# A two-layer decoder trunk on one core: output projection in 512 + 256 columns, sum of squares on GpSimd, two orders changed

## The chip, the core and the metric

The kernel runs on one core of a Trainium2 chip. A core has five engines that work side by side, each through its own queue: TensorE (PE; its weight loads are shown apart, as PEld), VectorE (DVE), ScalarE (ACT), GpSimd (POOL) and SyncE (SP), which here only issues DMAs. Matmuls read SBUF and write PSUM; DVE and ACT read both. The metric is the device time of one execution in microseconds, lower being better.

## The reference

The input x is 256 tokens of 1024 channels, float32. Each of two layers is a feed-forward block, a token mixer and a second feed-forward block, each on the RMS-normalised x and added back to it:

```python
def hybrid_layer(x, ...):
    x = x + 0.5 * swiglu(rms_norm(x, ffn1_norm), ffn1_w_gate_up, ffn1_w_down)
    h = rms_norm(x, mix_norm)
    z = h @ w_in                       # 512 pool, 3 x 512 attention, 2 x 1024 gate channels
    ...
    y_pool = multiscale_pool(u, pool_w, pool_scale)
    q = rope(rms_norm(q.reshape(B, S, N_HEADS, HEAD_DIM), q_norm))
    k = rope(rms_norm(k.reshape(B, S, N_HEADS, HEAD_DIM), k_norm))
    y_attn = moba_attention(q, k, v)
    gates = jax.nn.sigmoid(gl + b_gate).reshape(B, S, N_BRANCH, D)
    merged = gates[:, :, 0] * (y_pool @ w_branch_pool) + gates[:, :, 1] * (y_attn @ w_branch_attn)
    x = x + merged @ w_out
    x = x + 0.5 * swiglu(rms_norm(x, ffn2_norm), ffn2_w_gate_up, ffn2_w_down)
    return x
```

With 256 tokens there is one attention block, so the attention is a causal softmax over all keys, with 8 heads of 64. The hidden width of a feed-forward block is 2816.

## The kernel before

**Layout.** x lies as channels on 128 partitions by 256 tokens, in 8 columns of 128 channels (`x[:, f, :]`, f = 0 to 7; the tile is called `gx`). Weights stream from memory in units of 128 x 2048 float32 (`fetch`, line 96): one DMA on SP into `raw` (four buffers), then `split` (line 114) for each half: ACT writes the rounded high part `hi` (L115), DVE the remainder `lo` (L116). Six buffers each of `hi` and `lo` hold three units.

**Products.** Every float32 product is made from split operands in three terms: high weight by high data, high weight by low data, low weight by high data. Data that is split lies as `[P, 2, S]`, high half and low half side by side. `chain` (line 134) makes a product in two matmuls: the high weight by both halves (512 columns, the two results kept in two halves of a PSUM bank), and the low weight by the high half (256 columns, added to the first half). Its result is spread over two halves that a drain adds up. `chain3` (line 139) makes it in three matmuls of 256 columns that all add into one half.

**Order.** The order on PE is that of the program (`keep`). On the other engines a planner orders instructions by the program and by when their operands are ready.

**The norm.** RMS normalisation is taken out of the products: `prep(f, ...)` (line 237) is called for each column of x when it is finished. `split_x` writes the split column times its gain into `hx` (L225 on ACT, L226 on DVE), and `square_x` (line 228) squares it on ACT (L234) and adds it to `acc` on DVE (L235). `factor_spread` (line 274) splits `acc` into `ar` (`halves`, L187 and L188), sums it over the partitions with two matmuls (`ss`, L283) and takes the reciprocal root; the results are scaled later. A block that follows the mixer runs twelve steps of `columns` (four matmuls each) before `ss`, seven of them before column 7 of `hx` is needed. In the mixer, `factor` does the same with another matmul (`st`), after the first quarter of the projections.

**The start.** The first block takes its first three units in small pieces as they arrive (lines 682 to 697), and `pairs` (line 172) walks over them together, two rows of weights at a time. A row of `columns` (line 146) makes, for j = 0 and 1, a high and a low product.

**Attention.** Eight `gate` steps (line 491), each 32 matmuls over one weight unit, carry the attention between them (loop at line 602). `score_two` writes the scores of two pairs of heads into two PSUM tiles `sc`; on its second call, in the middle of `gate(4)`, it first writes the values' products of the first two pairs into a free part of the same two tiles (`ys`, `values_two`). `soften` runs `softmax` (line 428) on one `sc`: mask, maximum, exponential on ACT, and scaling by the sums (L448), which gives `pr`. `heads_end` (line 560) takes a values' product out of PSUM as a high half (L562, ACT) and a low half (L563, DVE) into `yk`, part of the tile `ax`. `turn_two` (line 581) allocates two tiles `pt`, which take over the buffers of `sc` (two buffers in this stage), then runs on PE four `pool_map` matmuls in each (on its second call) and six transposes of `pr` in each (L455).

**After the gates.** `branch` and `mixed` make the gated sum and split it into `mk` (`halves`). `project` (line 668) multiplies it by the output weights: eight columns f of eight products, the first three columns taken six products ahead. It then adds the column to x (L676, DVE) and calls `after(f)`, which is `prep` of the next block. Each column has a PSUM tile `ps` of two halves (`quarter`, four buffers), of which the first half is used.

`add_x` (line 359) drains a column of the down projection, made by `chain`: an ACT copy of the second half (L363), a DVE addition of it to x (L364), and a DVE addition of the first half out of PSUM (L365).

Of the kernel before, what the change touches and what calls it, by code (L numbers as in the profile page):

```python
# [18 lines left out]
F32 = mybir.dt.float32  # L19
F32R = mybir.dt.float32r  # L20
AF = mybir.ActivationFunctionType
OP = mybir.AluOpType
# [3 lines left out]
P = 128  # L26
D = 1024
S = 256
L = 2
NK = D // P  # L30
# [18 lines left out]
def trunk_kernel(ctx: ExitStack, tc: tile.TileContext, x_in, w_in, pw_in, qkn_in, rope_in, mask_in, band_in, out):  # L49
    nc = tc.nc  # L50
# [6 lines left out]
    small = ctx.enter_context(tc.tile_pool(name="small", bufs=4))  # L57
# [3 lines left out]
    def quarter(name):  # L61
        return pat.tile([P, 2, S], F32, name=name, tag="at")
# [10 lines left out]
    act = nc.scalar.activation  # L73
    tt = nc.vector.tensor_tensor
# [3 lines left out]
    def mm(*args, **kw):  # L78
        return keep(nc.tensor.matmul(*args, **kw))  # L79

    def banks(pool, name):

        return pool.tile([P, 2, 2, S], F32, name=name, tag="mm" if pool is pmm else "at2")
# [6 lines left out]
    def unit():  # L90

        if not ahead:
            fetch()
        return ahead.pop(0)
# [23 lines left out]
    def blk(z, b, n=1):  # L118

        size = z[0].shape[-1]  # L120
        c = b * P % size
        return z[b * P // size][:, c:c + n * P]

    def steps(z):

        if len(z.shape) == 3:
            z = z.rearrange("p a s -> p (a s)")
        return z.rearrange("p (s a c) -> p a s c", a=4, c=4)

    def prod(ps, w, xk, first, last):  # L130

        return mm(steps(ps), lhsT=w, rhs=steps(xk), start=first, stop=last)

    def chain(ps, hi, lo, b, xk, first, last):

        prod(ps, blk(hi, b), xk, first, False)
        return prod(ps[:, 0, :], blk(lo, b), xk[:, 0, :], False, last)

    def chain3(ps, hi, lo, b, xs, first=True, last=True):

        for i, xk in enumerate(xs):
            prod(ps, blk(hi, b + i), xk[:, 0, :], first and i == 0, False)
            prod(ps, blk(hi, b + i), xk[:, 1, :], False, False)
            prod(ps, blk(lo, b + i), xk[:, 0, :], False, last and i == len(xs) - 1)

    def columns(w, ps, ks):

        for k in ks:
            for j in range(2):
                chain(ps[j] if isinstance(ps, list) else ps[:, j], *w, 2 * k + j, hk[k], k == 0, k == NK - 1)  # L150

    def pair(w, t, other=None, at=0):

        ps = banks(pmm, "ps")
        columns(w, ps, range(at))
        if other:
            other()
        columns(w, ps, range(at, NK))
        drain(t, ps)
# [3 lines left out]
    def drain(t, ps):  # L163
        act(t, ps[:, :, 1, :], AF.Copy)  # L164
        drained.append(tt(t, ps[:, :, 0, :], t, op=OP.add))  # L165
# [6 lines left out]
    def pairs(ws, ts):  # L172

        pss = [banks(pmm, "ps"), banks(pmm, "ps"), *([quarter("pe") for _ in range(2)] for _ in ts[2:])]
        for k0 in range(0, NK, 2):
            for w, ps in zip(ws, pss):
                columns(w, ps, (k0, k0 + 1))
        for t, ps in zip(ts[:2], pss):
            drain(t, ps)
        for t, ps in zip(ts[2:], pss[2:]):  # L180
            for j, pe in enumerate(ps):
                act(t[:, j, :], pe[:, 1, :], AF.Copy)
                tt(t[:, j, :], pe[:, 0, :], t[:, j, :], op=OP.add)
# [9 lines left out]
    x = gx[:, L * NG:L * NG + NK * S].rearrange("p (k s) -> p k s", s=S)  # L193
# [25 lines left out]
    hk = [hx[:, k] for k in range(NK)]  # L219
    acc = acts.tile([P, S], F32, name="acc")  # L220

    def split_x(f, l, col):

        g = gain[:, l, col + f:col + f + 1]
        act(hx[:, f, 0, :], x[:, f, :], AF.Copy, scale=g)  # L225
        stt(hx[:, f, 1, :], x[:, f, :], g, hx[:, f, 0, :].bitcast(F32), op0=OP.mult, op1=OP.subtract)  # L226

    def square_x(f):

        if f == 0:  # L230
            act(acc, x[:, f, :], AF.Square)
        else:
            sq = small.tile([P, S], F32, name="sq", tag="sq", bufs=2)
            act(sq, x[:, f, :], AF.Square)  # L234
            tt(acc, acc, sq, op=OP.add)  # L235

    def prep(f, l, col):
        split_x(f, l, col)
        square_x(f)

    def rsqrt(r, ss, inv):

# [140 lines left out]
    def normed(pt, rt, name):  # L383
        z = acts.tile([P, 2, GW], F32, name=name, **({"tag": "v"} if name == "v" else {"tag": "tok", "bufs": 2}))
        for t in range(2):
            act(z[:, t, :], pt[:, t], AF.Copy, scale=rt[:, t:t + 1])
        return z
# [78 lines left out]
    def by_half(z):  # L466
        return z.rearrange("p (i c) -> p i c", c=P)

    def mix(l, after):
# [6 lines left out]
        k = normed(pt, rt, "k")  # L476
# [14 lines left out]
        def gate(f, *other):  # L491
            pair(unit(), gates[f], *other)
            fetch()

        def open_gate(f):
            tt(gates[f], gates[f], bc2(r), op=OP.mult)  # L496
            for j in range(2):
                c = j * NK + f
                act(gates[f][:, j, :], gates[f][:, j, :], AF.Tanh, scale=0.5, bias=hb[:, c:c + 1])
# [60 lines left out]
        def heads_end(p, y):  # L560

            act(by_half(yk[p][:, 0, :]), y, AF.Copy)  # L562
            tt(by_half(yk[p][:, 1, :]), y, by_half(yk[p][:, 0, :]).bitcast(F32), op=OP.subtract)  # L563
# [3 lines left out]
        scs, ys, prs = [], [], []  # L567
# [4 lines left out]
        def score_two(p):  # L572

            scs[:] = [flat("sc") for _ in range(2)]
            if p:
                ys[:] = [sc[:, :, rest] for sc in scs]
                values_two(0, ys)
            for i, sc in enumerate(scs):
                scores(qT, kT, p + i, sc)

        def turn_two(p, gs=()):

            pts = [flat("pt") for _ in range(2)]
            for g, pt in zip(gs, pts):
                pool_map(g, pt[:, :, rest])
            for pr, pt in zip(prs, pts):
                by_key(pr, pt)
            for pT, pt in zip(pTs[p:], pts):
                act(pT[:, :, :3 * P], pt[:, :, :3 * P], AF.Copy)
            for g, pt in zip(gs, pts):  # L590
                map_end(g, pt[:, :, rest])
            prs.clear()
# [6 lines left out]
        def soften(i, pin=False):  # L599
            prs.append(softmax(scs[i], pin))  # L600

        for h in range(NH):
            gate(h, *((lambda: score_two(h // 2), NK // 2) if h % 4 == 0 else ()))
            if h == 4:
                for i in range(2):
                    soften(i, i > 0)
                for p, y in enumerate(ys):
                    heads_end(p, y)
            elif h < 2:
                soften(h)  # L610
            elif h % 4 == 2:
                turn_two(h // 4 * 2, (0, 1) if h > 4 else ())
            elif h == 3:
                pool_diff()
            open_gate(h)
# [15 lines left out]
        ws = [unit() for _ in range(2)]  # L631
        two = [banks(pmm, "two") for _ in range(2)]
        sums = {0: two[0][:, 0], 2: two[1][:, 0]}
# [4 lines left out]
        ys = [y[:, :, :P] for y in both]  # L638
# [11 lines left out]
        mk = acts.tile([P, NK, 2, S], F32R, name="mk", tag="ga")  # L650
        mk = [mk[:, i] for i in range(NK)]
# [14 lines left out]
        ws, sums = [], []  # L666

        def project(f, k0=0, k1=NK):
            if f % 2 == k0 == 0:
                ws.append(unit())  # L670
            if k0 == 0:
                sums.append(quarter("ps"))
            ps = sums[f][:, 0]
            chain3(ps, *ws[f // 2], f % 2 * 8 + k0, mk[k0:k1], k0 == 0, k1 == NK)
            if k1 == NK:
                tt(x[:, f, :], ps, x[:, f, :], op=OP.add)  # L676
                after(f)

        for step in ((0, 0, 6), (1, 0, 6), (2, 0, 6), (0, 6), (1, 6), (2, 6), *((f,) for f in range(3, NK))):
            project(*step)  # L680
# [17 lines left out]
    for f in range(NK):  # L698
        square_x(f)
    n_unit[0] = len(w3)  # L700
    ahead.extend(w[1:] for w in w3)
    for l in range(L):
        ffn(lambda f: prep(f, l, C_GM), len(w3) if l == 0 else 0)
        if l == 0:
            for d, z in ((rope, rope_in), (mask, mask_in), (qkn, qkn_in)):
                nc.sync.dma_start(d, z)
        mix(l, lambda f: prep(f, l, C_G2))
        if l + 1 < L:
            ffn(lambda f: prep(f, l + 1, C_G1))
        else:  # L710
            ffn(lambda f: nc.sync.dma_start(out[:, f, :], x[:, f, :]), end=True)
# [90 lines left out]
```

## Time and profile before

| | |
|---|---|
| median of three runs | 1003.99 us (1003.69 to 1004.67) |
| profiled execution | 1004.1 us |
| its span, first to last instruction | 1002.2 us |
| granted TensorE clock | 1.000 |
| busy: PE, PEld | 997.2 us, 906.0 us |
| busy: DVE, ACT, POOL | 793.1 us, 619.5 us, 1.5 us |
| read from memory | 190.82 MB, 191 GB/s over the span |

Busy time of PE contains waiting inside its pipeline, so a busy PE alone proves nothing; its starts and the chain of work that ended last say more. In the timelines a row is: start in us, length in us, engine, line, operation, what it writes and reads, how many were merged, and in brackets how long the engine had been idle and what released it. In the groups, the numbers behind the bar are busy time, mean length in ns of one, and idle time before them with what ended it. In the chain of work a row is start, length, engine, tile, line and count. In a list of waits it is the total, the number and the longest.

### The profile page before, as it was taken

What the parts mean: (1) busy time and instruction counts of PE and PEld (TensorE: products, weight loads), DVE (VectorE), ACT (ScalarE), POOL (GpSimd) and SP (SyncE); (2) the same over time, 40 slices, a digit from 0 to 9 for tenths busy, and PEclk for the clock granted to TensorE, in tenths of its full rate; (3) what the DMA queues carried; (4) which work ended last, traced back from release to release, by engine and by line L of the source; (5) the groups of instructions that cost most, each with busy time, mean ns of one, the idle gap of its engine ahead of it and who ended that gap; (6) DMA issues with size and microseconds to landing.
All of it is one profiled execution on the core that took longest, in us unless ns stands there. A gap on an engine that the chain in (4) does not pass through costs nothing.

```text
span 1002.2 us, 16011 instructions
## 1 busy us (share of the span) xinstructions
PE 997.2 (100%) x6348; PEld 906.0 (90%) x6348; DVE 793.1 (79%) x1195; ACT 619.5 (62%) x981; POOL 1.5 (0%) x26
## 2 busy tenths in 40 slices
PE   9999999999999999999999999999999999999998
PEld 8888899898899998888889999888989999888898
DVE  6998866698978888886688888666989888888752
ACT  7866655557756666665575666556677567666541
POOL 0000000000000000000000000000000000000000
PEclk9999999999999999999999999999999999999999
DMA  8866655643546665565556566555545465565640
GB/s 294 314 210 210 209 186 195 221 157 146 191 139 210 207 212 174 206 210 189 193 190 212 184 209 206 183 201 191 188 176 172 131 215 202 187 204 198 205 152 22
DMA packets 30170, 192.89 MB, mean 192 GB/s; under 512 B 3344, under 2 KB 4624, under 8 KB 7568
## 3 DMA queue, kind: packets, MB, share of 16 engines
q1 hardware_dynamic: 30096, 191.88, 56.1%
q8 instruction: 49, 0.80, 0.3%
q14 instruction: 25, 0.20, 0.1%
HBM read 190.82 MB, written 1.05 MB: 191 GB/s over the span
## 4 chain that ended last, share of the span: by engine, by line
PE 97%; DVE 2%; DMA 0%; issue 0%; ACT 0%; SPq 0%
PE ps L79 83%; PE pt L79 7%; PE two L79 4%; PE pe L79 1%; PE sc L79 1%; DVE lo L116 1%; PE pt L455 1%; PE y L79 1%; DMA raw<-w 0%; PE tp L417 0%; DVE gates L165 0%; DVE gates L496 0%; DVE nb L438 0%; PE st L79 0%; DVE uT L538 0%; DVE gates L522 0%
## 5 line engine op out<-in xcount | busy, mean ns | idle before, releaser
L79 PE MATMUL ps<-hx,hi 128*128 128x512 f32 x1696 | 568.5, 383 | 0.4 <-ACT hi L115 0.4
L116 DVE TENSOR_TENSOR lo<-raw,hi 128x1024 fp32r<-128x1024 f32 (+2 forms) x372 | 440.1, 1187 | 136.1 <-ACT hi L115 130.9
L115 ACT ACTIVATE hi<-raw 128x1024 fp32r<-128x1024 f32 (+2 forms) x372 | 381.5, 1031 | 242.9 <-PE ps L79 185.2
L79 PE MATMUL ps<-hx,lo 128*128 128x256 f32 x1696 | 463.3, 273 | 0.0
L79 PEld LDWEIGHTS ps<-hx,hi 128*128 128x128 f32 x1696 | 318.5, 188 | 57.4 <-ACT hi L115 0.7
L79 PEld LDWEIGHTS ps<-hx,lo 128*128 128x128 f32 x1696 | 318.8, 188 | 0.2 <-DVE lo L116 0.2
L79 PE MATMUL ps<-ga,hi 128*128 128x512 f32 (+1 forms) x264 | 87.0, 376 | 0.0
L79 PE MATMUL ps<-gc,hi 128*128 128x512 f32 (+1 forms) x264 | 87.0, 376 | 0.0
L79 PE MATMUL ps<-ga,lo 128*128 128x256 f32 x256 | 69.9, 273 | 0.0
L79 PE MATMUL ps<-gc,lo 128*128 128x256 f32 x256 | 69.9, 273 | 0.0
L79 PE MATMUL ps<-gb,hi 128*128 128x512 f32 (+1 forms) x198 | 65.6, 376 | 0.0
L79 PE MATMUL pt<-hi,hx 128*128 128x512 f32 x192 | 64.9, 384 | 0.0
L338 DVE TENSOR_TENSOR ab<-ab,r 128x512 f32<-128x512 f32 x88 | 60.3, 689 | 2.2
L165 DVE TENSOR_TENSOR ab<-ps,ab 128x512 f32<-128x512 f32 x86 | 59.1, 687 | 2.0
L79 PEld LDWEIGHTS ps<-ga,hi 128*128 128x128 f32 x264 | 49.0, 188 | 8.3
L79 PEld LDWEIGHTS ps<-gc,hi 128*128 128x128 f32 x264 | 49.0, 188 | 8.3
L342 ACT ACTIVATE sg<-ab 128x256 f32<-128x256 f32 x88 | 36.2, 417 | 26.5 <-DVE ab L338 24.7
L79 PE MATMUL pt<-lo,hx 128*128 128x256 f32 x192 | 52.5, 274 | 0.0
L79 PE MATMUL ps<-gb,lo 128*128 128x256 f32 x192 | 52.4, 273 | 0.0
L164 ACT ACTIVATE ab<-ps 128x512 f32<-128x512 f32 x86 | 49.9, 580 | 0.0
L79 PEld LDWEIGHTS ps<-gc,lo 128*128 128x128 f32 x256 | 48.1, 188 | 0.0
L79 PEld LDWEIGHTS ps<-ga,lo 128*128 128x128 f32 x256 | 48.1, 188 | 0.0
(150 smaller groups left out, 1013.6 us busy)
## 6 DMA issues: line engine op xcount, KB each, us to landing
raw<-w SPq DMA_DIRECT2D x176, 1024.0 KB, 5.0
raw<-w SPq DMA_DIRECT2D x16, 256.0 KB, 5.3
out_dram<-gx SPq DMA_DIRECT2D x8, 128.0 KB, 2.1
gx<-x SPq DMA_DIRECT2D x3, 256.0 KB, 5.9
qk<-pw SPq DMA_DIRECT2D x2, 256.0 KB, 2.7
gx<-x SPq DMA_DIRECT2D x1, 300.0 KB, 2.8
qkn<-qkn SPq DMA_DIRECT2D x1, 256.0 KB, 7.5
rope<-rope SPq DMA_DIRECT2D x1, 128.0 KB, 4.9
```

Of the source, the lines that this page charges most:

```text
L79: return keep(nc.tensor.matmul(*args, **kw))
L115: act(hi, w, AF.Copy)
L116: tt(lo, w, hi.bitcast(F32), op=OP.subtract)
L164: act(t, ps[:, :, 1, :], AF.Copy)
L165: drained.append(tt(t, ps[:, :, 0, :], t, op=OP.add))
L338: scaled = tt(ab, ab, bc2(r[0]), op=OP.mult)
L342: act(sg, ab[:, 0, :], AF.Silu)
L455: keep(nc.tensor.transpose(pt[:, h, o * P:(o + 1) * P], pr[:, h, c * P:(c + 1) * P], ident))
```

## The change

The output projection uses `chain` in place of `chain3`, and its drain adds the two halves of the tile. `prep` hands GpSimd's addition to `square_x`; the sum of squares at the start of the kernel, outside `prep`, stays on DVE. In the step behind `gate(4)` the two `heads_end` stand ahead of the two `soften`. `pairs` begins with `opening`: for its first unit and first row, the two high products (j = 0 and 1), then the two low ones.

```diff
+    def opening(w, ps):
+
+        for j in range(2):
+            prod(ps[:, j], blk(w[0], j), hk[0], True, False)
+        for j in range(2):
+            prod(ps[:, j, 0, :], blk(w[1], j), hk[0][:, 0, :], False, False)
...
+        opening(ws[0], pss[0])
         for k0 in range(0, NK, 2):
             for w, ps in zip(ws, pss):
-                columns(w, ps, (k0, k0 + 1))
+                columns(w, ps, range(k0 if k0 or ps is not pss[0] else 1, k0 + 2))
...
-    def square_x(f):
+    def square_x(f, add=tt):
...
-            tt(acc, acc, sq, op=OP.add)
+            add(acc, acc, sq, op=OP.add)
...
     def prep(f, l, col):
         split_x(f, l, col)
-        square_x(f)
+        square_x(f, nc.gpsimd.tensor_tensor)
...
             if h == 4:
+                for p, y in enumerate(ys):
+                    heads_end(p, y)
                 for i in range(2):
                     soften(i, i > 0)
-                for p, y in enumerate(ys):
-                    heads_end(p, y)
...
-            ps = sums[f][:, 0]
-            chain3(ps, *ws[f // 2], f % 2 * 8 + k0, mk[k0:k1], k0 == 0, k1 == NK)
+            ps = sums[f]
+            for k in range(k0, k1):
+                chain(ps, *ws[f // 2], f % 2 * 8 + k, mk[k], k == 0, k == NK - 1)
             if k1 == NK:
-                tt(x[:, f, :], ps, x[:, f, :], op=OP.add)
+                t = small.tile([P, S], F32, name="t", tag="sg", bufs=2)
+                act(t, ps[:, 1, :], AF.Copy)
+                tt(t, t, x[:, f, :], op=OP.add)
+                tt(x[:, f, :], ps[:, 0, :], t, op=OP.add)
                 after(f)
```

## The prediction

> **What bounds the kernel now.** I read the page first: its heading, the busy times, the chain that ended last.
>
> ```profile
> span 1002.2 us, 16011 instructions
> ...
> PE 997.2 (100%) x6348; PEld 906.0 (90%) x6348; DVE 793.1 (79%) x1195; ACT 619.5 (62%) x981; POOL 1.5 (0%) x26
> ...
> PE 97%; DVE 2%; DMA 0%; issue 0%; ACT 0%; SPq 0%
> ```
>
> TensorE (PE) carries 97% of the chain, so only two things can change the time: how long PE's own instructions take, and how long it waits. The view of PE's waits has three rows, one of them for the warm-up before the first data. These are the other two:
>
> ```profile
> PE ps L79 <- ACT hi L115: 0.4, 1, 0.4
> PE pt L79 <- DVE ax L563: 0.2, 1, 0.2
> ```
>
> Very little waiting can be taken away, and much could be added: DVE, 79% busy, feeds PE through weight parts, the softmaxes, the gated sums and the norm. The next view, the chain in order of time, gives PE's rate by kind of product.
>
> ```profile
> 30.82 152.02 PE ps L79 x912
> ...
> 285.28 19.26 PE two L79 x168
> ...
> 304.54 30.02 PE ps L79 x240
> 334.56 0.23 PE ss L79 x2
> ...
> 800.36 30.02 PE ps L79 x240
> ```
>
> In the first row matmuls of 512 and of 256 columns alternate: 152.02 / 912 = 0.1667 us each, 0.3334 us for a pair. In the second all have 256 columns and three make a product: 19.26 / 168 = 0.1146, 0.344 for the three. Both forms stream 768 columns.
>
> **Part 1: the output projection.** `project` now calls `chain`, so 64 products in each layer have two matmuls in place of three: 128 matmuls and 128 weight loads go. The row at 304.54 holds the 192 matmuls of the old projection and 48 of the feed-forward block behind it (12 steps of `columns` with four each, before the sum of squares `ss`). Those 48 take 48 x 0.1667 = 8.00 us, the projection 22.02, or 0.3440 a product. The saving is 0.3440 - 0.3334 = 0.0106 us a product, **1.36 us** over 128. Layer 1 has the same row at 800.36. The columns are the same before and after, so the ends are 0 (only the columns count) and 1.36; I take 1.36, since the pair's rate comes from 912 matmuls of exactly the new form.
>
> The Trainium skill, page "TensorE: Matmul & The Clock Gate", section "Wait — 56ns, not 53.3ns?", gives a warm matmul its columns at 2.4 GHz plus about 2.5 ns. By it a matmul less saves 2.5 ns, an estimate of 0.3 us for the 128. The rows show 10.6 ns a product, and they are used.
>
> The first matmul of a product now takes both halves of `mk`, so it needs DVE's low half one matmul earlier. The last halves come in this order:
>
> ```profile
> 304.26 0.42 DVE L188 TENSOR_TENSOR mk<-mg,mk 128x256 fp32r<-128x256 f32 x1
> ...
> 308.47 0.41 DVE L188 TENSOR_TENSOR mk<-mg,mk 128x256 fp32r<-128x256 f32 x1
> ```
>
> The first of them is `mk[5]`, ready at 304.68; the projection reaches it after five products, at about 304.4 + 5 x 0.334 = 306.1. `mk[7]` is ready at 308.88 and comes after 18 products and one more, at 310.7. Both are hidden, with 1.4 us left.
>
> Each column's drain changes from one DVE addition out of PSUM to an ACT copy and two DVE additions, as `add_x` does already; the sums go to GpSimd (POOL), so a DVE addition leaves as one comes:
>
> ```profile
> L363 ACT ACTIVATE t<-ps 128x256 f32<-128x256 f32 x31 | 11.7, 376 | 17.5 <-PE ps L79 17.5
> L364 DVE SCALAR_TENSOR_TENSOR t<-t,gx 128x256 f32<-128x256 f32 x31 | 13.1, 421 | 7.0 <-ACT t L363 7.0
> L235 DVE TENSOR_TENSOR acc<-acc,sq 128x256 f32<-128x256 f32 x42 | 17.5, 417 | 0.0
> ```
>
> For ACT that is 16 x 0.376 = 6.0 us more in all. For DVE it is 16 x 0.42 more for the drain and 35 x 0.42 less for the sums. PE waits for neither as long as the norm's sum comes in time; that is the next part.
>
> **Part 2: the sum of squares on POOL.** The trace has no two-input POOL operation. The nearest row has one input and half as many elements:
>
> ```profile
> 1.71 0.29 POOL masks.py:199 TENSOR_SCALAR_AFFINE_SELECT ident<-ident 128x128 f32<-128x128 f32 x1
> ```
>
> Twice the elements make 0.58 us, twice the inputs again 1.16: the upper end. The lower end is DVE's 0.42. I take 0.6, nearer to the row. Alone this is hidden: in feed-forward blocks a column of 22 pairs takes 22 x 0.3334 = 7.3 us, and seven additions have that much time each. The tight place is behind the output projection, where a column takes 8 x 0.3334 = 2.67 us. Its rows on DVE:
>
> ```profile
> 314.76 0.42 DVE L676 TENSOR_TENSOR gx<-ps,gx 128x256 f32<-128x256 f32 x1
> ...
> 316.96 0.42 DVE L676 TENSOR_TENSOR gx<-ps,gx 128x256 f32<-128x256 f32 x1
> ...
> 319.16 0.41 DVE L676 TENSOR_TENSOR gx<-ps,gx 128x256 f32<-128x256 f32 x1
> ...
> 326.89 0.41 DVE L676 TENSOR_TENSOR gx<-ps,gx 128x256 f32<-128x256 f32 x1
> ...
> 331.38 0.42 DVE L188 TENSOR_TENSOR ar<-acc,ar 128x256 fp32r<-128x256 f32 x1
> ```
>
> The first is column 2, drained about 2.1 us after PE had finished it (304.4 + 24 x 0.344 = 312.7). DVE then needs 2.20 us a column (319.16 - 316.96) against PE's 2.67, and has caught up at column 7. The split sum `ar` ends at 331.80, and PE takes it at 334.56: **2.76 us of slack**. The longer drain and the slower addition cost about 0.38 + 0.18 plus a hand-over, say 0.7. The slack covers it: cost 0, ends 0 and the price of the second rival below.
>
> **Part 3: the values' parts ahead of the softmaxes.** `pt` takes over the buffers of `sc`, and the last reader of `sc` is `heads_end`'s subtraction (L563), which DVE does late. On PE:
>
> ```profile
> 271.82 0.60 PE L79 MATMUL pt<-uT,qk 128*128 128x128 f32 x4
> 272.61 0.71 PE L79 MATMUL pt<-uT,qk 128*128 128x128 f32 x4 [0.18 <-DVE ax L563]
> 273.15 1.47 PE L455 MATMUL pt<-ident,pr 128*128 128x128 f32 x12
> 274.38 0.47 PE L79 MATMUL ps<-hx,hi 128*128 128x512 f32 x1
> ...
> 767.80 1.35 PE L79 MATMUL pt<-uT,qk 128*128 128x128 f32 x8
> ...
> 770.22 0.47 PE L79 MATMUL ps<-hx,hi 128*128 128x512 f32 x1
> ```
>
> Eight group maps and twelve transposes last 2.56 us in layer 0 and 2.42 in layer 1. Undisturbed they need 0.92 and 1.23, from the starts of the same work elsewhere and of what follows it:
>
> ```profile
> 245.98 1.47 PE L455 MATMUL pt<-ident,pr 128*128 128x128 f32 x12
> 247.21 0.47 PE L79 MATMUL ps<-hx,hi 128*128 128x512 f32 x1
> ...
> 284.12 1.16 PE L79 MATMUL y<-uT,qk 128*128 128x128 f32 x8
> 285.04 0.47 PE L79 MATMUL two<-ax,hi 128*128 128x256 f32 x2
> ```
>
> So 0.41 and 0.27 us stand still, 0.68 in all. With L563 ahead of the softmaxes that wait goes. What is late next is the second softmax's scaling (L448), which the last six transposes read:
>
> ```profile
> 272.47 1.01 DVE L448 TENSOR_TENSOR pr<-pr,su 128x512 f32<-128x512 f32 x2
> ...
> 768.31 1.01 DVE L448 TENSOR_TENSOR pr<-pr,su 128x512 f32<-128x512 f32 x2
> ```
>
> The view of busy time by stage has a row for the stretch in which the softmaxes lie; after the name come its length, and then PE, PEld, DVE, ACT and POOL:
>
> ```profile
> 254.00:274.60 20.60, 20.42 (x151) 18.16 (x150) 20.20 (x42) 14.30 (x35) 0.00 (x0) 1.00 0.44 144
> ```
>
> DVE is busy for 20.20 of 20.60 us, so two subtractions done earlier delay what follows them and leave L448's end where it is: 273.48 and 769.32. Undisturbed, PE would want it at 271.82 + 0.92 + 0.62 = 273.36, and at 769.34. A hand-over of some 0.05 leaves waits of 0.17 and 0.03, so 0.24 and 0.24 are won: **0.48 us**, ends 0 and 0.68.
>
> **Part 4: both first high products ahead of the low ones.** This touches one place, the opening of the kernel:
>
> ```profile
> 5.62 0.80 PE L79 MATMUL ps<-hx,hi 128*128 128x512 f32 x1 [0.36 <-ACT hi L115]
> ...
> 6.08 0.29 PEld L79 LDWEIGHTS ps<-hx,lo 128*128 128x128 f32 x1 [0.17 <-DVE lo L116]
> ...
> 6.22 0.45 PE L79 MATMUL ps<-hx,lo 128*128 128x256 f32 x1
> ```
>
> The first wait is for the first high part and stays. The second, 0.17, is a weight load's; the matmul in front of it was still streaming for part of that. Ends 0 and 0.17; I take 0.06.
>
> **The sum.** 1.36 + 0.48 + 0.06 = 1.90 us. The profiled execution took 1004.1 (span 1002.2 and 1.9 around it); the median of the three runs is 1003.99, 0.1 below. From the median: **1002.1 us**. A measurement of this kernel tells about 0.2%, 2.0 us, from no change, so the forecast lies next to that line.
>
> **Rivals.** First, *the values' parts give nothing*: the softmax takes over the wait whole, or the planner puts its work later. For it speaks that L448 ends only 0.1 us from where PE wants it; against it that DVE's work there is the same in amount. 1004.0 - 1.36 - 0.06 = 1002.6.
>
> Second, *POOL's additions hold up DVE behind the projection*. If each takes b us from DVE, the five columns from 2 to 7 add 5b to its lateness there (its spare 0.47 a column goes into catching up the 2.1), and PE stands for 5b + 0.7 - 2.76 in each layer. That decides from b = 0.41 on. With b = 0.6 it is 0.94, 1.9 for two layers: the gain is gone, 1004.0.
>
> The Trainium skill, page "SBUF — State Buffer", section "Who interferes with whom", says that a VectorE instruction with two SBUF inputs and a GpSimd instruction that reads SBUF exclude each other, the second to start waiting until the first ends. L116, L226 and the new drain's first addition are such instructions. By that rule b is the whole addition; no run here shows it yet.
>
> Third, **the other side**, the same mechanism at its upper end: b = 1.16 makes 3.74 a layer, 7.5 in all, 1004.0 - 1.9 + 7.5 = 1009.6. It becomes slower by over 0.2% when 2 x (5b - 2.06) - 1.9 exceeds 2.0, from b = 0.80 on. For it speaks the two-input step that the POOL row lacks; against it, that the additions of one column need not meet DVE at a bad moment each time, and that the drain's second addition reads PSUM.
>
> Fourth, *everything at its best end*: 1.36 + 0.68 + 0.17 = 2.21, 1001.8.
>
> **How the numbers follow.** Forecast (1001.7 to 1002.4 with the ends of parts 3 and 4) 0.50; the values' parts give nothing 0.13; POOL takes the gain back, wholly or partly (1002.4 to 1006) 0.17; slower 0.10; best end 0.10. Over 0.2% faster means below 1001.98: the best end and about half of the forecast's width, with the runs' own scatter (1003.69 to 1004.67), 0.36. Slower 0.10, the rest 0.54. The range goes from 1001.4, the best end less scatter, to 1004.6, which leaves out the slower case and the worse part of the second rival.
>
> **What would show it.** Part 1: the projection's row with 128 matmuls a layer in 21.3 us, not 22.0. Part 2: POOL with 35 additions of about 0.6; `ss` without a wait, DVE's last `L188 ar` no later than 2.7 us behind its present distance to the projection's end. Part 3: no wait of `pt` for L563, at most 0.2 for L448. Part 4: the second high product right behind the first, no load waiting for L116. Wrong would be: POOL additions of 0.8 us and more with DVE's rows stretched or waiting beside them, or a wait of PE for `ar`, `hx` or `mk`.

## The result, and the profile after

| | before | changed |
|---|---|---|
| median | 1004.04 us (6 runs, 1003.69 to 1005.75) | 1011.84 us (6 runs, 1009.78 to 1016.24) |
| again, later | 1004.11 us (18 runs) | 1009.27 us (4 runs, 1008.45 to 1010.23) |
| profiled execution, its span | 1004.1, 1002.2 us | 1016.24, 1014.2 us |

The changed kernel is slower: ratio 1.0083, interval 1.0069 to 1.0097 in the first comparison, 1.0050 (1.0032 to 1.0068) in the second. The profiled execution is the slowest of its six, so the profile holds some time that the median does not; it is sorted out below.

The page of the changed kernel, heading, busy times, chain and the group of the sums (behind the bars: busy time, mean ns of one, idle time before them):

```profile
span 1014.2 us, 15830 instructions
...
PE 1005.2 (99%) x6220; PEld 904.2 (89%) x6220; DVE 803.0 (79%) x1176; ACT 623.8 (62%) x997; POOL 33.6 (3%) x61
...
PE 94%; DVE 3%; ACT 1%; DMA 0%; issue 0%; SPq 0%
...
L243 POOL TENSOR_TENSOR acc<-acc,sq 128x256 f32<-128x256 f32 x35 | 32.2, 919 | 800.4 <-ACT sq L242 800.3
```

128 PE instructions are gone (6220 against 6348), and the span is 12.0 us longer. PE's part of the chain fell from 97% to 94%, and DVE's rose from 2% to 3%: the end now hangs, for a while, on DVE. The 35 additions on POOL last 919 ns on average.

The view of PE's waits (total us, number, longest), the row that is new:

```profile
PE ps L79 <- DVE hx L234: 3.8, 5, 1.4
```

`hx` is the split and scaled column of x that the feed-forward block behind the mixer reads. The chain in order of time (start, length, engine, tile, line, count) shows where it is late. Layer 0, from the start of the output projection to the sum of squares, and then the rows that matter later:

```profile
5.90 5.00 PE ps L79 x16
...
306.22 23.90 PE ps L79 x143
330.12 0.95 DVE hx L234
331.07 0.33 DVE gx L688
331.40 1.13 DVE lo L116
332.54 0.87 DVE hx L234
333.41 0.34 DVE t L687
...
334.12 1.22 DVE lo L116
335.33 0.89 DVE hx L234
...
336.27 2.32 PE ps L79 x12
338.59 0.23 PE ss L79 x2
...
838.10 0.23 PE ss L79 x2
838.34 172.53 PE ps L79 x1030
```

PE runs without a stop until it wants column 5 and then waits for one `hx` after the other: columns 5, 6 and 7. (The chain leaves PE behind 143 matmuls, where the split begins that PE will wait for.) The stage lasts 338.59 - 306.22 = 32.37 us, 30.02 before. In layer 1 it goes from 804.88 to 838.10, 33.22 us. Where the four long differences lie:

| stretch | before | changed | difference |
|---|---|---|---|
| start of PE plus first 16 matmuls | 5.62 + 3.44 | 5.90 + 5.00 | +1.8 |
| output projection to `ss`, layer 0 | 30.02 | 32.37 | +2.35 |
| the same, layer 1 | 30.02 | 33.22 | +3.20 |
| last 1030 matmuls | 168.27 | 172.53 | +4.26 |

The first and the last row are not in the second profile of the same kernel (`a1_changed_again`: 3.01 and 168.25 us) though the code is the same; without them this execution would have taken 1016.24 - 1.8 - 4.26 = 1010.2, and that profile's was 1009.89. What both profiles of the changed kernel have is in the two middle rows.

### The profile page after: what moved, and what is told of

The parts are those of the page before. It is cut to its first block, busy times and chain, and to the rows that moved or that the text cites. A ratio compares the mean times of both kernels' runs of the same rounds, so it can differ in the third digit from the quotient of the medians.

```text
span 1014.2 us, 15830 instructions
## 1 busy us (share of the span) xinstructions
PE 1005.2 (99%) x6220; PEld 904.2 (89%) x6220; DVE 803.0 (79%) x1176; ACT 623.8 (62%) x997; POOL 33.6 (3%) x61
## 4 chain that ended last, share of the span: by engine, by line
PE 94%; DVE 3%; ACT 1%; DMA 0%; issue 0%; SPq 0%
PE ps L79 81%; PE pt L79 6%; PE two L79 4%; PE pe L79 1%; DVE lo L116 1%; ACT pr L451 1%; PE y L79 1%; DVE hx L234 0%; PE pt L463 0%; DMA raw<-w 0%; PE tp L425 0%; PE sc L79 0%; DVE uT L546 0%; DVE gates L172 0%; ACT hi L115 0%
## 5 line engine op out<-in xcount | busy, mean ns | idle before, releaser
L79 PE MATMUL ps<-hx,hi 128*128 128x512 f32 x1696 | 575.4, 386 | 4.4 <-DVE hx L234 3.8
L115 ACT ACTIVATE hi<-raw 128x1024 fp32r<-128x1024 f32 (+2 forms) x372 | 381.0, 1030 | 238.2 <-PE ps L79 180.4
L243 POOL TENSOR_TENSOR acc<-acc,sq 128x256 f32<-128x256 f32 x35 | 32.2, 919 | 800.4 <-ACT sq L242 800.3
```

The lines of the kernel that those rows point to most:

```text
L115: act(hi, w, AF.Copy)
L243: add(acc, acc, sq, op=OP.add)
```

## What was asked of the chip

Two theories to begin with. **A**: POOL's additions take time from DVE, so `hx` comes late. **B**: the new drain, over ACT and with two DVE additions, makes `hx` late. When the drain turned out to matter, two more about it. **C**: it is the hop over ACT. **D**: it is the second addition on DVE. The table says when the low half of column 7 of `hx` was ready in layer 0, counted from the first matmul of the projection; PE wants it after 64 x 0.3334 + 36 x 0.1667 = 27.3 us with the new projection. (Of the twelve steps of `columns`, nine lie ahead of the first use of column 7, not seven as the section on the kernel before says; columns 5 and 6 are wanted after five and six steps, at 24.7 and 25.3.)

| kernel | sums on | projection, drain | column 7 ready, us | stage to `ss`, us | median, us |
|---|---|---|---|---|---|
| before | DVE | old | 24.8 | 30.02 | 1004.1 |
| e2 | POOL | old | 25.8 | 30.02 | 1004.58 |
| a2 | DVE | new, two DVE additions | 26.7 | 29.33 | 1002.58 |
| a3 | DVE | new in four columns, over ACT | 25.8 | 29.68 | 1003.30 |
| e1 | DVE | new, over ACT | 27.5 | 29.71 | 1003.85 |
| b1 | POOL | new, two DVE additions | 28.9 | 31.05 | 1008.37 |
| a4 | DVE | new, over ACT, one addition on POOL | 30.1 | 32.3 | 1008.67 |
| changed | POOL | new, over ACT | 30.2 | 32.37 | 1009.27, 1011.84 |

**e1_sums_on_dve.** The sums go back to DVE.

```diff
-        square_x(f, nc.gpsimd.tensor_tensor)
+        square_x(f)
```

> The changed kernel with the sums of squares back on DVE; all else as changed. In the changed kernel PE waits in the steps behind the output projection for L234 (the low halves of hx), three times and 2.6 us in all in each layer, and then runs 3.4 us at half the granted clock once. Theory A (POOL takes time from DVE: L234 beside an addition lasts 0.95 us where it lasted 0.48): without POOL on that work the waits go, L234 is back at 0.48, and the time is 1002 to 1004. Theory B (the longer drain is the cause: column 0's t waits on ACT behind a weight split and its first DVE addition behind another, so x of column 0 is done 2.9 us later in the stage than before): the waits stay, since DVE gets seven additions of 0.34 in each layer back and loses about as much stretching; PE waits 1.5 us or more in each layer and the time is 1007 to 1011.

1003.85 us (10 runs), ratio 1.0001 (0.9991 to 1.0010). Nearly the whole loss goes with POOL's additions, as A says. But the gain of the projection doesn't come: the stage lasts 29.71 us where 29.33 were to be had, column 7 is 2.7 us later than before, and PE's weight loads wait for `hx` four times, 0.9 us in all. So B's drain is there too. Its rows, on ACT and then on DVE:

```profile
310.94 1.06 ACT L115 ACTIVATE hi<-raw 128x1024 fp32r<-128x1024 f32 x1 [3.25 <-PE ps L79]
311.91 0.64 ACT L686 ACTIVATE t<-ps 128x256 f32<-128x256 f32 x2
```

```profile
312.04 1.23 DVE L116 TENSOR_TENSOR lo<-raw,hi 128x1024 fp32r<-128x1024 f32 x1 [3.33 <-ACT hi L115]
313.18 0.75 DVE L687 TENSOR_TENSOR t<-t,gx 128x256 f32<-128x256 f32 x2
313.85 0.75 DVE L688 TENSOR_TENSOR gx<-ps,t 128x256 f32<-128x256 f32 x2
```

The copy of the first two columns (L686) stands behind the split of a weight part on ACT, and DVE's additions then stand behind the other half of that split. Before, DVE took column 0 out of PSUM as soon as PE had finished it.

**e2_old_projection.** The sums stay on POOL, projection and drain are the old ones.

```diff
-            ps = sums[f]
-            for k in range(k0, k1):
-                chain(ps, *ws[f // 2], f % 2 * 8 + k, mk[k], k == 0, k == NK - 1)
+            ps = sums[f][:, 0]
+            chain3(ps, *ws[f // 2], f % 2 * 8 + k0, mk[k0:k1], k0 == 0, k1 == NK)
...
-                t = small.tile([P, S], F32, name="t", tag="sg", bufs=2)
-                act(t, ps[:, 1, :], AF.Copy)
-                tt(t, t, x[:, f, :], op=OP.add)
-                tt(x[:, f, :], ps[:, 0, :], t, op=OP.add)
+                tt(x[:, f, :], ps, x[:, f, :], op=OP.add)
```

> The changed kernel with the output projection and its drain as before; the sums stay on POOL. Theory A (POOL): L234 still lasts up to 0.95 us beside additions, PE still waits for hx behind the projection, 1007 to 1011. Theory B (drain): DVE's work behind the projection is that of before plus about 0.5 us a column and minus 0.34, which the 2.8 us of slack cover; no wait of PE for hx, no drop of the granted clock, 1003 to 1004.5, the projection's stage 30.0 us as before.

1004.58 us (10 runs), 0.1 above B's range, ratio 1.0004 (0.9995 to 1.0014): POOL's additions alone cost nothing that can be measured, although beside them DVE's instructions last longer. One of them on POOL, then DVE:

```profile
322.35 0.74 POOL L243 TENSOR_TENSOR acc<-acc,sq 128x256 f32<-128x256 f32 x1 [2.75 <-ACT sq L242]
```

```profile
322.41 0.96 DVE L234 SCALAR_TENSOR_TENSOR hx<-gx,hx 128x256 fp32r<-128x256 f32 x1
...
324.76 0.97 DVE L234 SCALAR_TENSOR_TENSOR hx<-gx,hx 128x256 fp32r<-128x256 f32 x1
```

The split of `hx` (L234) starts 0.06 us behind the addition and lasts 0.96 us; alone it lasts 0.48. A column takes DVE 324.76 - 322.41 = 2.35 us. Column 7 is ready 1.0 us later than before, and there was room for it. Neither A nor B alone makes the loss.

**e3_no_opening** and **e4_values_late** undo one of the two orders each (`pairs` without `opening`; the two `heads_end` behind the two `soften`).

```diff
-        opening(ws[0], pss[0])
...
-                columns(w, ps, range(k0 if k0 or ps is not pss[0] else 1, k0 + 2))
+                columns(w, ps, (k0, k0 + 1))
```

> The changed kernel without the opening: each first high product is followed by its low one, as before. In the changed kernel's trace the clock rises to full 10.2 us after the start, before it rose at 6.6 us, and the first 16 matmuls take 5.00 us against 3.44. If the opening causes that, the first 16 take about 3.4 us again and the time falls by 1.5 us. If it is the place of the clock's window, which differs from one execution to the next, the first 16 take 3.4 us or 5.0 us whatever the order, and the median moves by less than the runs' scatter.

```diff
-                for p, y in enumerate(ys):
-                    heads_end(p, y)
                 for i in range(2):
                     soften(i, i > 0)
+                for p, y in enumerate(ys):
+                    heads_end(p, y)
```

> The changed kernel with the values' parts behind the softmaxes again. From gate 3 to gate 7 the stretch on PE was 27.17 and 27.03 us before (layers 0 and 1) and 27.06 and 27.06 in the changed kernel: the move has won 0.1 us at most, since the wait for L563 became one for the second softmax's scaling. So: 27.2 and 27.0 again, PE waits for L563, and no difference in the time that can be measured against the changed kernel. If the move had won the 0.48 us that the prediction gave it, this kernel would be 0.5 us slower than the changed one.

1010.03 us, ratio 1.0059 (1.0044 to 1.0074), and 1009.43, ratio 1.0056 (1.0040 to 1.0073), four runs each. Beside the changed kernel's 1.0050 on the same chip neither order makes a difference that shows. The first 16 matmuls of e3 take 3.21 us, but those of e1, which has `opening`, 2.96: the 5.00 of the first profile don't come from `opening`.

**a1_changed_again** is the changed kernel as it is, for a second profile.

> The changed kernel as it is, beside the next three on one chip. So far neither part alone is slow (sums back on DVE 1003.85, old projection 1004.58), and without the opening or with the values' parts late it is 1010.03 and 1009.43. If waits of PE behind the projection are the whole cause, PE waits in each layer again for L234 three times, the two stages last 32.3 us or more against 30.02 before, and the time is at least 1004.0 + 2 x 2.3 = 1008.7, more by 1.7 us for each window of 3.4 us in which the granted clock halves after a wait.

1009.27 us, ratio 1.0050. Its two stages last 32.31 and 33.16 us, as in the first profile; the first matmuls and the last 1030 are undisturbed.

**a2_dve_drain.** Sums on DVE, and a drain without ACT: DVE adds both halves out of PSUM.

```diff
-        square_x(f, nc.gpsimd.tensor_tensor)
+        square_x(f)
...
-                t = small.tile([P, S], F32, name="t", tag="sg", bufs=2)
-                act(t, ps[:, 1, :], AF.Copy)
-                tt(t, t, x[:, f, :], op=OP.add)
-                tt(x[:, f, :], ps[:, 0, :], t, op=OP.add)
+                for j in (1, 0):
+                    tt(x[:, f, :], ps[:, j, :], x[:, f, :], op=OP.add)
```

> Sums on DVE, projection in 512 + 256 columns, but each column is drained by two DVE additions out of PSUM with no ACT copy between. Counted from the projection's first matmul, the low half of hx of column 7 was done after 24.8 us in the kernel before, 25.8 with POOL's sums alone, 27.5 with the new drain alone (sums on DVE) and 30.2 in the changed kernel; PE needs it at 28.0 (old projection) or 27.3 (new). Theory C (the hop over ACT: the first columns' copies wait behind a weight split on ACT, and their additions behind another on DVE): without the hop it is done by 26.5, no wait is left, the stage lasts 29.34 and the time is 1002.6. Theory D (the amount of DVE's work: 2.8 us a column against PE's 2.67): the same number of DVE additions, so it is done at 27.2 to 27.6 again, some 0.3 us of waits a layer are left, and the time stays at 1003.3 to 1003.9.

1002.58 us (10 runs), ratio 0.9991 (0.9981 to 1.0001); PE waits for no `hx`, and the stage has its 29.33 us. Column 7 is ready at 26.7, between what C and D expected: of the 2.7 us that the new drain costs in e1, 1.9 stay without ACT. Both are at work: C takes 2.2 us of column 0 (ready at 11.9 in e1, 9.7 here and before), D grows from column to column. DVE's rows for one column:

```profile
320.60 0.49 DVE L234 SCALAR_TENSOR_TENSOR hx<-gx,hx 128x256 fp32r<-128x256 f32 x1
321.00 0.43 DVE L243 TENSOR_TENSOR acc<-acc,sq 128x256 f32<-128x256 f32 x1
321.33 0.76 DVE L686 TENSOR_TENSOR gx<-ps,gx 128x256 f32<-128x256 f32 x2
322.00 1.23 DVE L116 TENSOR_TENSOR lo<-raw,hi 128x1024 fp32r<-128x1024 f32 x1
323.13 0.49 DVE L234 SCALAR_TENSOR_TENSOR hx<-gx,hx 128x256 fp32r<-128x256 f32 x1
```

DVE is never idle here, and from one L234 to the next it needs 323.13 - 320.60 = 2.53 us: 0.40 for the split, 0.33 for the sum, 0.67 for two additions out of PSUM, 1.13 for a weight part, start to start.

**a3_four_columns.** Only columns 3 to 6 in the new form, and only they with the drain over ACT; sums on DVE.

```diff
-            for k in range(k0, k1):
-                chain(ps, *ws[f // 2], f % 2 * 8 + k, mk[k], k == 0, k == NK - 1)
+            if f in (3, 4, 5, 6):
+                for k in range(k0, k1):
+                    chain(ps, *ws[f // 2], f % 2 * 8 + k, mk[k], k == 0, k == NK - 1)
+            else:
+                chain3(ps[:, 0], *ws[f // 2], f % 2 * 8 + k0, mk[k0:k1], k0 == 0, k1 == NK)
```

> Sums on DVE; only columns 3 to 6 of the projection use 512 + 256 columns and the longer drain, columns 0, 1, 2 and 7 are as before. Both theories of the drain let the low half of hx of column 7 be done at about 26 us after the projection's start, before PE needs it (27.7), so no wait is left; half of the projection's gain is kept: stage 29.68 against 30.02, time 1003.3. If the gain of 10.6 ns a product is not there at all, the stage is 30.02 and the time 1004.0.

1003.30 us (10 runs), ratio 0.9994 (0.9984 to 1.0003), and a stage of 29.68 us, both as expected. The time alone would not tell it from the kernel before; the stage does: half the products give half the gain, and with column 0 free of the hop nothing waits.

**a4_drain_on_pool.** Sums on DVE, but the drain's first addition goes to POOL.

```diff
-                tt(t, t, x[:, f, :], op=OP.add)
+                nc.gpsimd.tensor_tensor(t, t, x[:, f, :], op=OP.add)
```

> Sums on DVE; projection in 512 + 256 columns; the drain's first addition (t + x, both in SBUF) is on POOL. DVE has as many instructions behind the projection as before the change. Theory A with the size now seen (a DVE instruction with two SBUF inputs lasts 0.48 us longer beside a POOL addition of 0.74): hx of column 7 at 24.8 + 7 x 0.15 to 7 x 0.48 plus the hop, 26 to 28.5 us; waits between none and 1.2 us a layer; time 1002.6 to 1005. Theory D (the amount of DVE's own work alone) has it at 25 to 26, no waits, 1002.6.

1008.67 us (4 runs), ratio 1.0047 (1.0031 to 1.0063), column 7 at 30.1: outside the expectation. In its waits:

```profile
PE ps L79 <- DVE hx L234: 4.1, 6, 1.3
```

Here x itself waits for POOL, whose additions stand behind DVE's splits of weights and last 0.89 to 1.73 us one by one. POOL on the way to `hx` costs about as much as POOL beside it with the same drain (30.1 and 30.2 us).

**b1_dve_drain_pool_sums.** The changed kernel with the drain of a2.

```diff
-                act(t, ps[:, 1, :], AF.Copy)
-                tt(t, t, x[:, f, :], op=OP.add)
-                tt(x[:, f, :], ps[:, 0, :], t, op=OP.add)
+                for j in (1, 0):
+                    tt(x[:, f, :], ps[:, j, :], x[:, f, :], op=OP.add)
```

> The changed kernel with one edit: each column of the projection is drained by two DVE additions out of PSUM, with no ACT copy; the sums of squares stay on POOL. hx of column 7 was done 24.8 us after the projection's start before, 25.8 with POOL's sums, 27.5 with the drain over ACT, 26.7 with the DVE drain, 30.2 with POOL's sums and the drain over ACT. If the two causes add up (DVE's spare time is gone, and each second on POOL costs DVE 0.48 a column, less 0.34 for the addition that leaves), the DVE drain with POOL's sums is done at 26.7 + 1.0 = 27.7 to 28.5, 0.4 to 1.2 us late for PE (27.3): 1003.4 to 1005. If the hop over ACT is what POOL's sums make worse, it is 27.3 or less, no waits, 1002.6.

1008.37 us (4 runs), ratio 1.0041 (1.0028 to 1.0055), column 7 at 28.9, 0.4 later than the expectation's end, and a time 3.4 us above it. The four runs lie in two pairs, at 1007.2 and at 1009.5 to 1009.9, and the profiled one, of the upper pair, holds 3.3 us more than before in the 912 matmuls of the first block (155.32 for 152.02), far from the projection. The stage is the surer figure: 31.05 us in both layers, 1.72 above the 29.33 of a2, where the changed kernel's 32.37 is 3.04 above. So the hop over ACT isn't needed for the loss, but adds to it. One column on DVE:

```profile
318.96 0.96 DVE L234 SCALAR_TENSOR_TENSOR hx<-gx,hx 128x256 fp32r<-128x256 f32 x1
319.85 0.74 DVE L686 TENSOR_TENSOR gx<-ps,gx 128x256 f32<-128x256 f32 x2
320.51 1.21 DVE L116 TENSOR_TENSOR lo<-raw,hi 128x1024 fp32r<-128x1024 f32 x1
321.64 0.95 DVE L234 SCALAR_TENSOR_TENSOR hx<-gx,hx 128x256 fp32r<-128x256 f32 x1
...
331.69 0.96 DVE L234 SCALAR_TENSOR_TENSOR hx<-gx,hx 128x256 fp32r<-128x256 f32 x1
332.57 0.41 DVE L686 TENSOR_TENSOR gx<-ps,gx 128x256 f32<-128x256 f32 x1
332.90 1.21 DVE L116 TENSOR_TENSOR lo<-raw,hi 128x1024 fp32r<-128x1024 f32 x1
334.03 0.41 DVE L686 TENSOR_TENSOR gx<-ps,gx 128x256 f32<-128x256 f32 x1
334.37 1.21 DVE L116 TENSOR_TENSOR lo<-raw,hi 128x1024 fp32r<-128x1024 f32 x1
335.50 0.94 DVE L234 SCALAR_TENSOR_TENSOR hx<-gx,hx 128x256 fp32r<-128x256 f32 x1
```

From 318.96 to 321.64 it takes 2.68 us, the 2.67 in which PE makes a column: DVE can't catch up any more. The last column has two weight parts ahead of its split, where a2 has one; that is 1.1 us more for column 7.

**b2_projection_alone.** The kernel before with nothing but the new projection and DVE's own drain.

```diff
-            ps = sums[f][:, 0]
-            chain3(ps, *ws[f // 2], f % 2 * 8 + k0, mk[k0:k1], k0 == 0, k1 == NK)
+            ps = sums[f]
+            for k in range(k0, k1):
+                chain(ps, *ws[f // 2], f % 2 * 8 + k, mk[k], k == 0, k == NK - 1)
...
-                tt(x[:, f, :], ps, x[:, f, :], op=OP.add)
+                for j in (1, 0):
+                    tt(x[:, f, :], ps[:, j, :], x[:, f, :], op=OP.add)
```

> The kernel before with one edit: the projection in 512 + 256 columns, drained by two DVE additions out of PSUM. No POOL, no opening, the values' parts late as before. If the projection's saving is all that the four edits are worth, the stages last 29.34 us and the time is 1004.05 - 1.36 = 1002.7, as with the other two edits in (1002.58). If the opening or the values' parts gave anything, it is slower than that by what they gave (at most 0.5).

1002.89 us (11 runs), ratio 0.9988 (0.9979 to 0.9997): faster than the kernel before, by 1.25 us, and than the changed one. Its stage in the chain:

```profile
304.76 29.33 PE ps L79 x176
334.10 0.23 PE ss L79 x2
```

a2, which has both orders besides, has 0.9991 (0.9981 to 1.0001): between these two nothing can be told apart.

**c1_pool_copy** and **c2_pool_memset** measure the meeting of POOL and DVE by itself: e2 with another POOL instruction in place of the addition, one that reads SBUF and one that only writes it. The sums of squares of the columns are left out.

```diff
-            add(acc, acc, sq, op=OP.add)
+            if add is tt:
+                add(acc, acc, sq, op=OP.add)
+            else:
+                nc.gpsimd.tensor_copy(sq, sq)
```

> The kernel with the old projection and POOL's sums, but POOL copies each squared column onto itself in place of adding it (one SBUF input in place of two). The sums of squares are left out inside the layers. Beside the addition of 0.74 us L234 lasted 0.96. If a POOL instruction that reads SBUF holds up a DVE instruction with two SBUF inputs until it ends, L234 lasts 0.48 plus what is left of the shorter copy when it starts: 0.6 to 0.8. If only two inputs against two inputs collide, it is 0.48.

```diff
-                nc.gpsimd.tensor_copy(sq, sq)
+                nc.gpsimd.memset(sq, 0.0)
```

> The same with a POOL memset of the squared column, which writes SBUF and reads nothing. The sums of squares are left out inside the layers. If only POOL's reads collide with DVE's second input, L234 lasts 0.48 beside it. If any POOL access does, it is longer by what is left of the memset when L234 starts, up to 0.3 us.

One profile each, of 1004.02 and 1004.36 us. POOL and DVE of the copy, then of the memset:

```profile
320.96 0.47 POOL L246 COPY sq<-sq 128x256 f32<-128x256 f32 x1 [2.33 <-ACT sq L242]
```

```profile
321.10 0.61 DVE L234 SCALAR_TENSOR_TENSOR hx<-gx,hx 128x256 fp32r<-128x256 f32 x1
```

```profile
320.84 0.31 POOL L246 MEMSET sq<- 128x256 f32 x1 [2.22 <-ACT sq L242]
```

```profile
320.98 0.48 DVE L234 SCALAR_TENSOR_TENSOR hx<-gx,hx 128x256 fp32r<-128x256 f32 x1
```

The copy lengthens the split by 0.13 us, the addition by 0.48, and the memset, which covers the split's start as well, by nothing. Copy and addition still had 0.33 and 0.68 us to go when the split began, so the split doesn't wait for the whole of it: 0.20 us are missing both times.

## Why the prediction failed

The forecast was 1002.1 us with a range to 1004.6; the changed kernel takes 1009.3 to 1011.8. By its steps:

**The projection's saving (Part 1)** holds. In a2 and b2 the stage is 30.02 - 29.33 = 0.69 us shorter, 1.38 for two layers where 1.36 was predicted, or 10.8 ns a product. The 2.5 ns of the Trainium skill ("TensorE: Matmul & The Clock Gate", "Wait — 56ns, not 53.3ns?") would have made 0.16 a layer, an estimate; here each matmul less is also a weight load less, and no run separates the two. No run shows a wait for `mk`.

**The step that failed is in Part 2: "DVE then needs 2.20 us a column (319.16 - 316.96) against PE's 2.67, and has caught up at column 7"**, and with it "The longer drain and the slower addition cost about 0.38 + 0.18 plus a hand-over, say 0.7. The slack covers it". The 2.20 was the kernel's before; it wasn't worked out again with the change in it. The drain was charged once, as a delay, but DVE has almost no idle time behind the projection (0.26 us before, between the splits of columns 0 and 7), so it pays for every column. Start to start, the runs show for one column on DVE:

| | split of `hx` | sum | drain | weight part | together |
|---|---|---|---|---|---|
| before | 0.39 | 0.34 | 0.34 | 1.13 | 2.20 |
| e2, sums on POOL | 0.88 | - | 0.34 | 1.13 | 2.35 |
| a2, new drain | 0.40 | 0.33 | 0.67 | 1.13 | 2.53 |
| b1, both | 0.88 | - | 0.67 | 1.13 | 2.68 |

Against the 2.67 us in which PE makes a column of the new projection, the spare time with which DVE makes up its lateness is 0.47, 0.32, 0.14 and nothing. (With the old projection, as before and in e2, PE takes 2.75, so that 0.08 more is left.) Each edit alone leaves some; together they leave none. That is why e1 and e2 both take the time of the kernel before, and why the two don't add up: column 7 comes 1.0 us later with POOL's sums, 2.7 with the new drain, 5.3 with both. With both, the drain over ACT makes column 0 2.2 us later at the start, and nothing wins it back. The rest of the 5.3 in the changed kernel comes from there on: from the start of column 0's split to that of column 7's it takes DVE 17.73 us, 15.08 before, with seven weight parts between them both times, and the last split itself is 0.48 longer.

**The place of the deadline** was wrong too. The slack of 2.76 us was counted at `ar`, for `ss`. But `hx` of columns 5 to 7 is wanted first: column 7 has 27.3 - 24.8 = 2.5 us, and PE stood at column 5 already. By lateness and slack of column 7 PE loses 5.3 - 2.5 = 2.8 us a layer; the stage became 32.37 - 29.33 = 3.04 us longer than it could have been.

**The rivals.** The second and the third had the mechanism, POOL against DVE, and the Trainium skill's rule ("SBUF — State Buffer", "Who interferes with whom") agrees in kind: additions and copies that began first lengthen L234, the memset doesn't. In size the split waits 0.20 us less than to the end, as c1 showed. Its price was b = 0.48 us a column (less 0.34 for the addition that DVE no longer makes, which the formula leaves out), below the 0.6 taken and below the 0.80 from which the third rival was to decide; by their formula 2 x (5 x 0.48 + 0.7 - 2.76) = 0.7 us would have been lost. The fault is in the other term, the 0.7 for the drain: 2.7 us at column 7 by itself. That the third rival's 1009.6 lies near the measured 1009.3 is luck: it rests on a b of 1.16, which wasn't there. The addition on POOL lasts 0.73 to 0.74 us undisturbed, where 0.6 was taken, and to 1.07 beside DVE; it is on nobody's way itself, since the last part of `ar` is ready 0.6 us behind the last `hx` (30.8 against 30.2 us).

**The values' parts (Part 3)** were to give 0.48 us. PE's rows of the stretch in layer 0 of the changed kernel:

```profile
273.63 1.05 PE L79 MATMUL pt<-uT,qk 128*128 128x128 f32 x8
274.51 1.81 PE L463 MATMUL pt<-ident,pr 128*128 128x128 f32 x12
276.08 0.47 PE L79 MATMUL ps<-hx,hi 128*128 128x512 f32 x1
```

It lasts 276.08 - 273.63 = 2.45 us, 2.56 before; in layer 1 it is 2.46 after 2.42. The wait for the subtraction is gone, and the next one has taken its place, as the section said, but at nearly its whole length. In the waits of the weight loads:

```profile
PEld pt L463 <- DVE pr L456: 0.7, 2, 0.4
```

L456 (L448 before) starts 0.75 us behind the first group map, 0.65 before. On DVE its reciprocals wait for the last exponential on ACT (273.67), and another instruction of the gates (L504) then goes ahead of it, until 274.38:

```profile
273.80 0.66 DVE L504 TENSOR_TENSOR gates<-gates,r 128x512 f32<-128x512 f32 x1
274.38 1.02 DVE L456 TENSOR_TENSOR pr<-pr,su 128x512 f32<-128x512 f32 x2
```

"Leave L448's end where it is" failed: this end isn't set by DVE's amount of work alone, but also by the order that the planner chose. In e4, with the values' parts late again, L504 goes earlier, L456 starts 0.49 us behind the first group map, and the stretch on PE lasts 2.43 and 2.44 us: the move wins nothing.

**The opening (Part 4)**, 0.06 us, can't be seen in any run: e3 takes no longer. The weight load's wait that it was to remove is still there in a1, 0.16 us after 0.17.

## What to carry to other kernels

Before an engine is given one more instruction per step, add up its step anew, in the stretch where it has to catch up, and compare it with the step of the engine that waits for it: as long as there is spare time an edit looks free, and the one that uses up the last of it pays for all. Look up every deadline of what it makes, not the last one, and count a hop to another in-order engine with the long instructions that stand ahead of it there. Of the two fastest versions here, a2 and b2, which can't be told apart, the smaller edit is the projection's new form alone, with its two halves added by DVE.

## What else the runs showed of the hardware

**A halved clock behind a short wait.** Behind the waits of layer 1 the granted clock halves. The view of busy time by stage of the changed kernel (length, then PE, PEld, DVE, ACT and POOL, granted clock, share of DMA, GB/s):

```profile
829.00:832.83 3.83, 2.18 (x12) 1.48 (x11) 3.80 (x7) 2.22 (x5) 1.18 (x2) 1.00 0.81 270
832.83:836.24 3.41, 3.41 (x13) 2.92 (x12) 2.46 (x4) 1.24 (x3) 0.73 (x1) 0.50 0.68 276
```

At half the clock for 3.41 us PE could do about 1.7 us less work, an estimate, some of which it would have waited anyway: layer 1 took 33.22 us, layer 0 32.37 with the same first two waits (0.24 and 1.41 us). `a1_changed_again` shows it in the same place; e3, e4, a4 and b1 have waits of 1.3 or 1.4 us and don't, so whether the wait causes it isn't shown. In a1 and e3 together the four runs with a mean granted clock of 0.998 took 1009.9 to 1011.4 us, the four with 0.999 or 1.000 took 1008.5 to 1009.1. The Trainium skill, page "TensorE: Matmul & The Clock Gate", section "What's actually happening", names windows of 3413 ns that run freely. The length agrees; but the page halves the clock after a window in which PE idles, and here PE worked for 2.18 of the 3.83 us before.

**A slow stretch at the full clock.** The first profile and the second, the same 161.7 us of each:

```profile
838.30:1000.00 161.70, 161.70 (x947) 142.91 (x946) 121.40 (x163) 91.91 (x132) 0.00 (x0) 1.00 0.51 174
```

```profile
838.30:1000.00 161.70, 161.70 (x980) 145.83 (x980) 120.12 (x163) 90.81 (x132) 0.00 (x0) 1.00 0.51 175
```

PE runs 947 matmuls in the one and 980 in the other, without idle time, at a granted clock of 1.00 in both. The figures of DVE, ACT and the DMAs are alike. b1's profile has a similar stretch from 66 to 186 us, far from the projection. What causes it stays open; it is 4.26 us of the first profile's 12.0.

**The start varies.** The first 16 matmuls took between 2.96 and 5.00 us in these profiles, with `opening` (3.86 in e2, 3.01 in a1) and without (3.44 before, 3.21 in e3, 3.94 in b2).
